# Two feed-forwards: GpSimd's products on the residual are put behind a copy that reads the last low part of x

## The chip, the cores and the metric

The kernel runs on one core of one Trainium2 chip. A core has a matrix engine (TensorE, PE in the profile, with its weight loads as PEld), a vector engine (VectorE, DVE), a scalar engine (ScalarE, ACT), GpSimd (POOL) and a queue engine that starts most transfers (SyncE, SP). The metric is the device time of one execution in microseconds (us).

## What is computed

Two layers of a decoder trunk on 512 tokens of width 1024, in float32. Each layer is a token mixer, a residual with a norm, a feed-forward, and again a residual with a norm:

```python
for i in range(DEPTH):                       # DEPTH = 2
    y = gla_mixer(h, ...) if i == 0 else gdn_mixer(h, ...)
    h = layer_norm(ALPHA * h + y, ln_g[i, 0], ln_b[i, 0])
    h = layer_norm(ALPHA * h + conv_ffn(h, ...), ln_g[i, 1], ln_b[i, 1])

def layer_norm(x, g, b):
    return (x - mean) * rsqrt(var + eps) * g + b

def conv_ffn(x, w_in, conv_w, w_out):        # 2 x 2816 columns
    gate, up = split(causal_dwconv(x @ w_in, conv_w))
    return (gelu(gate) * up) @ w_out
```

## The kernel before

**Number format.** TensorE is fed with two parts of each float32 number, a high part in a fast format (`xh`, `wh`) and a low part, the rest (`xl`, `wl`). A product is three matmuls: `xh` with `wh`, `xl` with `wh`, `xh` with `wl`. ScalarE makes the high part of a weight tile by a copy, and VectorE the low part by a subtraction (`split_out`, L732).

**Layout.** Tokens stand in four blocks of 128 (`tb`), the width in two halves of 512 columns (`hf`). The residual `h[tb][hf]` has tokens on the partitions. What the matmuls of the next stage read, `xh` and `xl`, has the width on the partitions, in eight chunks (`NC`), with all 512 tokens along the row.

**The norm (`ln`, L896 ff.).** It runs once for each block, when the mixer's output projection has added its sum into `h[tb]`. `ln_stats` makes mean and inverse root: statistics on VectorE (L884, L888), a square root on ScalarE (L886), and four small instructions on VectorE, one number for each partition (L892, L893, L894, L906). Then VectorE normalises half 0 (L908) and ScalarE half 1 (L907), TensorE transposes both (`xT`, L235), ScalarE multiplies by `g` and adds `b` on the way out of the accumulator (L925), one of the two engines writes `xh` (L929, L932), and VectorE writes `xl` (L933).

**The residual that is kept.** The `h` that the next residual needs is also to be multiplied by `g` and to get `b` added, with the columns along the row this time. After the mixers that is GpSimd's work: L949 multiplies `h[hf]` by a tile of `g` spread over all partitions, L950 adds the one of `b`, eight products and eight sums for each feed-forward. The four tiles of `g` and `b` (`gb`) are loaded by SyncE (L871) into slots of the feed-forward's stage. Nobody reads these `h` before the feed-forward's first group of output tiles is added into them, a hundred microseconds later. In the norm behind the first feed-forward (`spill`) the residual goes to memory instead, and GpSimd has no such work; behind the second the output is written.

**The start of a feed-forward.** TensorE's order is the program's. When the feed-forward begins (`fm_items`), the norms of blocks 2 and 3 are still to come: the first four column blocks of the weights (of 128 columns each, 24 matmuls) are first multiplied with tokens 0 to 255 only, matmuls of 128x256, and the transposes of blocks 2 and 3 stand in between, after the first 18 matmuls and after 18 more. Then the same four are multiplied with tokens 256 to 511, and from the fifth on a column block takes all 512 tokens at once. Behind each come ScalarE's first tap of the convolution out of the accumulator (L1037), two taps on VectorE (L1039), the gelu for a gate (L1057), and the product of gate and up (L1068). The weights go through four buffers of `wh` and `wl` (`WB`).

**Slots.** A feed-forward's stage has six slots of 128x512 (`FFN_SLOTS`), which the four `gb` tiles and the gates' `conv` tiles share. A tile that takes over a slot waits until its last reader has done.

**What sets the order.** The program issues the work from generators with a clock of its own, in which flags such as `("x", tb)` stand for finished steps. In `ln`, the GpSimd part of block `tb` is issued when all four flags of x are set and RESID_DELAY + 10 x `tb` of that clock have passed. The order in which an engine gets its instructions is then laid down by a planner that takes them when their data are ready by its own estimate; only TensorE's order is nailed to the program's. An engine runs its list in order, and each instruction waits, on the chip, for the data and tiles that it needs, whatever the program's clock had said. So a product of GpSimd can start as soon as its block is normalised and transposed and `g` has landed. `behind(a, b)` adds to the planner's rules that `a` comes after `b` on their engine; it adds no wait of its own.

Of the kernel before, what the change touches and what calls it, by code (L numbers as in the profile page):

```python
# [8 lines left out]
F32 = mybir.dt.float32  # L9
# [6 lines left out]
P = 128  # L16
D = 1024
S = 512
NTB = S // P
NC = D // P  # L20
# [50 lines left out]
def c4(t):  # L71
    return t.rearrange("p (c i) -> p c i", c=4)


def blk(i, n=P):
    return slice(i * n, i * n + n)


class Trunk:
# [818 lines left out]
    def ln(self, tb, spill=False):  # L898

        nc = self.nc  # L900
        li, h = self.li, self.h[tb]
        for hf in range(2):
            self.flags.pop(("h", tb, hf))
        mv, rs = self.ln_stats(tb)
        nb = self.small([P, 1], "ln_nb")
        nc.vector.scalar_tensor_tensor(nb, mv[:, 0:1], -1.0, rs, ALU.mult, ALU.mult)  # L906
        nc.scalar.activation(h[1], h[1], AF.Identity, bias=nb, scale=rs)  # L907
        normed = nc.vector.tensor_scalar(h[0], h[0], mv[:, 0:1], rs, op0=ALU.subtract, op1=ALU.mult)  # L908
        if self.due and tb < 2:
            if tb:  # L910
                self.behind(self.lows[3], normed)
            self.normed = normed
        ready = self.vec(0.65)
        yield ready - self.clk + 0.2
        for hf in range(2):
            ps = self.psum("xT")
            self.tr4(ps, h[hf])
            xf = self.slot("xf")
            for j in range(4):
                c = li * NC + 4 * hf + j  # L920
                if spill and hf and tb == NTB - 1:
                    nc.vector.tensor_scalar(xf[:, blk(j)], ps[:, blk(j)], self.lg[:, c:c + 1], self.lb[:, c:c + 1],
                                            op0=ALU.mult, op1=ALU.add)
                else:
                    nc.scalar.activation(xf[:, blk(j)], ps[:, blk(j)], AF.Identity,  # L925
                                         bias=self.lb[:, c:c + 1], scale=self.lg[:, c:c + 1])
            xs = (slice(None), slice(4 * hf, 4 * hf + 4), blk(tb))
            if hf == 0:
                nc.vector.tensor_copy(self.xh[xs], c4(xf))  # L929
                self.vec(0.42, self.clk + 1.8)  # L930
            else:
                nc.scalar.copy(self.xh[xs], c4(xf))  # L932
            nc.vector.tensor_sub(self.xl[xs], c4(xf), self.xh[xs])  # L933
            ready = self.vec(0.7, self.clk + (2.6 if hf else 0.0))
        self.set(("x", tb), max(0.1, ready - self.clk))
        yield 0.0

        self.spilled = spill
        if spill:
            for hf in range(2):  # L940
                nc.gpsimd.dma_start(self.hd[blk(tb), blk(hf, S)], h[hf])
            self.h[tb] = None
            return
        for i in range(NTB):
            yield from self.until(("x", i))
        yield RESID_DELAY + 10.0 * tb
        gb = self.ln_gb()
        for hf in range(2):
            nc.gpsimd.tensor_mul(h[hf], h[hf], gb[hf])  # L949
            nc.gpsimd.tensor_add(h[hf], h[hf], gb[2 + hf])  # L950
            self.set(("h", tb, hf))
            yield 5.0
# [1191 lines left out]
```

## Time and profile before

| | |
|---|---|
| median of the runs | 1217.89 us (1217.6 to 1219.16) |
| the profiled execution | 1219.53 us |
| its span, first to last instruction | 1217.8 us |
| granted clock of TensorE | 1.000 |
| first feed-forward's first matmul, second one's | 208.84 us, 855.56 us |
| GpSimd's products and sums (L949, L950), first feed-forward | 199.55 to 239.6 us |
| the same, second feed-forward | 854.31 to 888.9 us |

The page gives the busy time of each engine. The list of waits says who stood idle, and what ended it. A row of the timeline has the start in us, the length in us, the engine, the line of the kernel, the operation, the tile written and the tiles read, the shapes, and in brackets the idle time ahead of it with what ended that. Rows of the same kind that follow each other are drawn into one, with their count.

### The profile page before, as it was taken

To read this page: it belongs to the slowest core of one execution; us is meant where nothing else is said; L and a number is where in the kernel's file an instruction comes from. 1 tells how busy PE (TensorE), PEld (TensorE's weight loads), DVE (VectorE), ACT (ScalarE), POOL (GpSimd) and SP (SyncE) were. 2 spreads that over 40 slices of the span, in tenths; PEclk is the share of its full clock that TensorE was granted. 3 is DMA by queue.
4 is the path that set the end of the run, shared out by engine and by line. 5 is a ranking of instruction groups with operands and counts; after the bars stand their busy time and mean duration, and the time that the engine had idled before them with its cause. 6 is when DMAs were issued, how large, how long until landed. Compare 5 with 4: busy or idle time off the path is not lost.

```text
span 1217.8 us, 17218 instructions
## 1 busy us (share of the span) xinstructions
PE 1208.7 (99%) x6477; PEld 1020.4 (84%) x6477; DVE 928.2 (76%) x1527; ACT 628.3 (52%) x1116; POOL 170.9 (14%) x211
## 2 busy tenths in 40 slices
PE   9999999999999999999999999999999999999998
PEld 8888888988888888889888888988888888888886
DVE  6989787787757675766789969799697757775667
ACT  5666663544434443454678557864544433443440
POOL 3030101601100110001242032200610100020000
PEclk9999999999999999999999999999999999999999
DMA  8384652536743554433444356535444853383311
GB/s 234 111 168 112 136 155 71 186 109 138 190 121 94 123 95 121 127 99 90 122 127 130 90 136 105 118 125 143 154 119 106 180 164 102 103 176 88 112 60 69
DMA packets 177907, 152.55 MB, mean 125 GB/s; under 512 B 16966, under 2 KB 140938, under 8 KB 177824
## 3 DMA queue, kind: packets, MB, share of 16 engines
q1 hardware_dynamic: 161920, 115.23, 32.0%
q0 software_dynamic: 14944, 35.57, 15.3%
q8 instruction: 51, 0.84, 0.3%
q10 hardware_dynamic: 960, 0.66, 0.2%
q14 instruction: 32, 0.26, 0.1%
HBM read 133.06 MB, written 5.78 MB: 114 GB/s over the span
## 4 chain that ended last, share of the span: by engine, by line
PE 92%; DVE 5%; ACT 1%; DMA 1%; issue 1%; SPq 0%; DVEq 0%; POOL 0%; ACTq 0%; POOLq 0%
PE fm L217 51%; PE fold L217 22%; PE tm L217 11%; PE o L217 2%; DVE wl L732 1%; PE xT L235 1%; DVE conv L1640 1%; DVE tmp L1800 1%; PE pg L217 1%; PE vn L217 1%; PE yT L235 1%; DVE tt L1802 1%; PE V L217 0%; PE ds L217 0%; PE qs L217 0%
## 5 line engine op out<-in xcount | busy, mean ns | idle before, releaser
L217 PE MATMUL fm<-xh,wh 128*128 128x512 f32 (+2 forms) x1096 | 400.7, 368 | 0.7 <-ACT xh L732 0.7
L217 PE MATMUL fm<-xl,wh 128*128 128x512 f32 (+2 forms) x1096 | 399.0, 366 | 0.2 <-DVE xl L933 0.2
L217 PE MATMUL fm<-xh,wl 128*128 128x512 f32 (+1 forms) x1072 | 391.8, 367 | 0.0
L732 DVE TENSOR_TENSOR wl<-raw,wh 128x1024 fp32r<-128x1024 f32 (+1 forms) x156 | 195.0, 1252 | 139.3 <-ACT wh L732 139.2
L732 ACT CAST wh<-raw 128x1024 fp32r<-128x1024 f32 (+1 forms) x157 | 162.6, 1037 | 203.3 <-PE fm L217 124.4
L217 PEld LDWEIGHTS fm<-xh,wh 128*128 128x128 f32 (+1 forms) x1096 | 205.5, 188 | 34.0 <-ACT xh L732 0.9
L217 PEld LDWEIGHTS fm<-xl,wh 128*128 128x128 f32 (+1 forms) x1096 | 205.5, 188 | 33.2 <-DVE xl L933 0.5
L217 PEld LDWEIGHTS fm<-xh,wl 128*128 128x128 f32 x1072 | 201.3, 189 | 33.2
L1039 DVE SCALAR_TENSOR_TENSOR conv<-fm,ffn_cw,conv 128x511 f32<-128x511 f32 x112 | 83.5, 746 | 10.0 <-ACT conv L1037 8.4
L732 ACT CAST wh<-b 128x1024 fp32r<-128x1024 f32 x48 | 50.2, 1053 | 74.0 <-PE fold L217 34.0
L217 PE MATMUL fold<-wh,fh 128*128 128x512 f32 x224 | 87.7, 391 | 0.0
L217 PE MATMUL fold<-wl,fh 128*128 128x512 f32 x224 | 87.2, 390 | 0.0
L217 PE MATMUL fold<-wh,fl 128*128 128x512 f32 x224 | 87.2, 389 | 0.0
L732 DVE TENSOR_TENSOR wl<-b,wh 128x1024 fp32r<-128x1024 f32 x48 | 58.4, 1223 | 22.4 <-ACT wh L732 22.0
L417 POOL DMA_DIRECT2D b<-b x24 | 20.8, 915 | 354.6 <-DVE wl L732 309.9
L1057 ACT ACTIVATE conv<-conv 128x512 f32<-128x512 f32 x44 | 27.8, 631 | 66.0 <-DVE conv L1039 66.0
L1640 DVE SCALAR_TENSOR_TENSOR conv<-fm,gdn_cw,conv 128x511 f32<-128x511 f32 (+2 forms) x72 | 54.1, 789 | 8.1 <-ACT conv L1638 7.5
L217 PEld LDWEIGHTS fold<-wh,fh 128*128 128x128 f32 x224 | 42.1, 188 | 9.5 <-DVE h L1128 1.0
L217 PEld LDWEIGHTS fold<-wh,fl 128*128 128x128 f32 x224 | 42.1, 188 | 8.8
L217 PEld LDWEIGHTS fold<-wl,fh 128*128 128x128 f32 x224 | 42.1, 188 | 8.6
L1039 DVE SCALAR_TENSOR_TENSOR form<-fm,ffn_cw,form 128x511 f32<-128x511 f32 x64 | 47.7, 746 | 1.1
L217 PE MATMUL fold<-wh,xh 128*128 128x512 f32 x104 | 43.4, 417 | 0.2
(362 smaller groups left out, 2039.8 us busy)
## 6 DMA issues: line engine op xcount, KB each, us to landing
raw<-in_ffn_w_in_dram SPq DMA_DIRECT2D x88, 512.0 KB, 3.8
raw<-in_gdn_w_in_dram SPq DMA_DIRECT2D x28, 512.0 KB, 4.1
b<-in_ffn_w_out_dram SPq DMA_DIRECT2D x24, 512.0 KB, 5.8
b<-b POOLq DMA_DIRECT2D x24, 512.0 KB, 4.7
raw<-in_ffn_w_out_dram SPq DMA_DIRECT2D x20, 512.0 KB, 3.7
raw<-in_gla_w_in_dram SPq DMA_DIRECT2D x18, 512.0 KB, 4.1
gw<-in_gla_w_in_dram POOLq DMA_DIRECT2D x8, 512.0 KB, 7.2
raw<-in_gla_w_out_dram SPq DMA_DIRECT2D x8, 512.0 KB, 4.2
```

What stands on the lines that cost most here:

```text
L217: t = self.nc.tensor.matmul(out, a, b, start=start, stop=stop, skip_group_check=joined)
L235: t = self.nc.tensor.transpose(out, a, self.ident[:n, :n])
L417: self.nc.gpsimd.dma_start(out, group[src, i][:, cols], accum_op=ALU.add)
L732: return self.nc.scalar.copy(dst_h, src), self.nc.vector.tensor_sub(dst_l, src, dst_h)
L1039: nc.vector.scalar_tensor_tensor(a[:, d:], ps[:, :S - d], tap(2 - d), a[:, d:], ALU.mult, ALU.add)
L1057: nc.scalar.activation(a, a, AF.Gelu)
L1640: self.conv = nc.vector.scalar_tensor_tensor(a[:, d:], ps[:, :S - d], tap(3 - d), a[:, d:], ALU.mult, ALU.add)
L1800: nc.vector.tensor_tensor(tv, m3[:, j, j + 1:].unsqueeze(2).to_broadcast([P, n, m]), t3[:, j, :m].unsqueeze(1).to_broadcast([P, n, m]), AL ...
L1802: nc.vector.tensor_add(t3[:, j + 1:, :m], t3[:, j + 1:, :m], tv)
```

## The change

For block 0 the generator first issues a copy of one column, on GpSimd, into a small tile of its own. It reads the last token of the last chunk of `xl`, which the norm of block 3 writes (L933). Each of the eight products (L949) is placed behind this copy on GpSimd; the sums follow their products as before. It holds for the norms behind both mixers, so for both feed-forwards.

```diff
         gb = self.ln_gb()
+        if tb == 0:
+            self.gate = nc.gpsimd.tensor_copy(self.small([P, 1], "gate"), self.xl[:, NC - 1, S - 1:].bitcast(F32))
         for hf in range(2):
-            nc.gpsimd.tensor_mul(h[hf], h[hf], gb[hf])
+            self.behind(nc.gpsimd.tensor_mul(h[hf], h[hf], gb[hf]), self.gate)
             nc.gpsimd.tensor_add(h[hf], h[hf], gb[2 + hf])
```

## The prediction, on record before the result

> **What bounds the kernel now.** I read the page first, then who waited for whom on TensorE, then the timelines of the four engines around each start of a feed-forward. The page says where a gain can be at all:
>
> ```profile
> PE 1208.7 (99%) x6477; PEld 1020.4 (84%) x6477; DVE 928.2 (76%) x1527; ACT 628.3 (52%) x1116; POOL 170.9 (14%) x211
> ```
>
> TensorE is busy for 1208.7 of 1217.8 us. GpSimd, whose products are moved, is busy for 14% and never bounds by itself. So the change can only pay where GpSimd makes somebody late for whom TensorE then waits. The list of TensorE's waits, longest first, begins with
>
> ```profile
> PE xT L235 <- DVE h L908: 1.8, 1, 1.8
> ```
>
> one wait of 1.8 us of the transposes `xT` for the normalised residual `h`, written by VectorE at L908. The timeline puts it at 858 us, where the second feed-forward begins while the norm of its input is still running for the last two blocks of 128 tokens. VectorE there (start, us, engine, line):
>
> ```profile
> 846.57 0.22 DVE L893 SCALAR_TENSOR_TENSOR ln_t<-ln_rs,ln_var 128x1 f32<-128x1 f32 x1
> 846.82 0.16 DVE L894 SCALAR_TENSOR_TENSOR ln_rs<-ln_t,ln_rs 128x1 f32<-128x1 f32 x1
> 847.01 0.16 DVE L906 SCALAR_TENSOR_TENSOR ln_nb<-ln_mv,ln_rs 128x1 f32<-128x1 f32 x1
> 847.09 0.54 DVE L908 TENSOR_SCALAR h<-h,ln_mv,ln_rs 128x512 f32<-128x512 f32 x1
> ...
> 854.13 0.16 DVE L892 RECIPROCAL ln_rs<-ln_root 128x1 f32<-128x1 f32 x1 [0.42 <-ACT ln_root L886]
> 854.33 1.28 DVE L893 SCALAR_TENSOR_TENSOR ln_t<-ln_rs,ln_var 128x1 f32<-128x1 f32 x1
> 855.64 1.23 DVE L894 SCALAR_TENSOR_TENSOR ln_rs<-ln_t,ln_rs 128x1 f32<-128x1 f32 x1
> 856.79 0.68 DVE L933 TENSOR_TENSOR xl<-xf,xh 128x512 fp32r<-128x512 f32 x1
> 857.39 1.23 DVE L906 SCALAR_TENSOR_TENSOR ln_nb<-ln_mv,ln_rs 128x1 f32<-128x1 f32 x1
> 858.54 1.57 DVE L908 TENSOR_SCALAR h<-h,ln_mv,ln_rs 128x512 f32<-128x512 f32 x1
> ```
>
> The same four lines are there twice. For block 1 (from 846.57) they take 0.22, 0.16, 0.16 and 0.54 us; for block 2 (from 854.33) they take 1.28, 1.23, 1.23 and 1.57 us, with one element per partition in three of them. Data cannot explain that. GpSimd does: in just these microseconds it runs four of the products that the change moves.
>
> ```profile
> 854.31 5.52 POOL L949 TENSOR_TENSOR h<-h,gb 128x512 f32<-128x512 f32 x4 [63.71 <-DVE ln_rs L892]
> ```
>
> 5.52 us for four is 1.38 us each, so the products end at about 855.7, 857.1, 858.5 and 859.8, and VectorE's stretched instructions end at 855.6, 856.9, 858.6 and 860.1: VectorE gets on when a product ends. The Trainium skill (SBUF — State Buffer, section "Who interferes with whom") says that VectorE and GpSimd share one pair of SBUF ports and that whichever starts first holds it for its whole instruction; the ends above agree.
>
> **What is removed, in the second feed-forward.** TensorE there and, as the yardstick, at the start of the first feed-forward, where the same order of matmuls and transposes met no wait:
>
> ```profile
> 855.56 0.28 PE L217 MATMUL fm<-xh,wh 128*128 128x256 f32 x1
> ...
> 858.10 0.28 PE L217 MATMUL fm<-xh,wl 128*128 128x256 f32 x1
> 860.17 1.09 PE L235 MATMUL xT<-ident,h 128*128 128x128 f32 x8 [1.79 <-DVE h L908]
> ...
> 864.21 0.36 PE L217 MATMUL fm<-xh,wh 128*128 128x256 f32 x1
> ```
>
> ```profile
> 208.84 0.28 PE L217 MATMUL fm<-xh,wh 128*128 128x256 f32 x1
> ...
> 210.99 1.04 PE L235 MATMUL xT<-ident,h 128*128 128x128 f32 x8
> ...
> 214.80 0.36 PE L217 MATMUL fm<-xh,wh 128*128 128x256 f32 x1
> ```
>
> Between the first `fm` matmul and the third run of them (36 matmuls of 128x256 and 16 transposes) the second feed-forward takes 864.21 - 855.56 = 8.65 us, the first 214.80 - 208.84 = 5.96 us. The difference, **2.69 us**, is what the stall costs; it is more than the 1.8 us of the wait list, because starts count also a short wait for `xl` (written at 856.79) and a short one before the second transposes, and the list counts idle time against modelled ends. I take the 2.69.
>
> Does it all come back? Without products beside it block 2's chain starts at 854.13, when ScalarE's root is there (ScalarE is not touched), and takes 0.16 + 0.22 + 0.16 + 0.68 + 0.16 + 0.54 = 1.9 us: VectorE's half of `h` is done at about 856.1. The transposes want it at 855.56 + (210.99 - 208.84) = 857.71 and came at 860.17. So 1.6 us of cover stand where 2.46 us were missing; ScalarE's half, which starts when L906 ends, has a little less. What is late next is nothing on this path: block 3's norm follows 2.4 us earlier than before too.
>
> In the first feed-forward the products already end up between VectorE's instructions without making TensorE wait (5.96 us, the bare time): nothing to win there, 0.
>
> **What is added.** One copy of a 128x1 on GpSimd per feed-forward. The nearest row is the same instruction at the start of the kernel:
>
> ```profile
> L1366 POOL COPY gk<-xl 128x1 f32<-128x1 f32 x1 | 0.6, 582 | 4.0 <-DVE xl L732 4.0
> ```
>
> 0.58 us on an idle engine; at worst it holds VectorE for as long once, after the last `xl`, when VectorE has nothing to do until the next weight's cast. On the path 0.
>
> **What is moved.** All eight products and eight sums of a feed-forward now queue behind the copy on GpSimd. Nothing else is queued there: the next instructions of GpSimd are the additions of the folded weights, a whole group of tiles later. SyncE's loads of `gb`, and those of the weights behind them, wait for tiles that the norms free, not for GpSimd. The cost is that GpSimd finishes later, and two things look at that: VectorE, beside which it now runs longer, and the slots of `g` and `b`, which come free later. The rows of the second feed-forward's sixteen:
>
> ```profile
> L950 POOL TENSOR_TENSOR h<-h,gb 128x512 f32<-128x512 f32 x8 | 12.8, 1617 | 10.0 <-DMA gb<-in_ln_b_dram 10.0
> L949 POOL TENSOR_TENSOR h<-h,gb 128x512 f32<-128x512 f32 x8 | 12.0, 1531 | 63.7 <-DVE ln_rs L892 63.7
> ```
>
> 24.8 us in all, in either feed-forward. I work it through in the first, where TensorE's times will not move:
>
> ```profile
> 220.50 1.08 DVE L933 TENSOR_TENSOR xl<-xf,xh 128x512 fp32r<-128x512 f32 x1 [0.90 <-ACT xh L932]
> ...
> 236.83 3.90 DVE L732 TENSOR_TENSOR wl<-raw,wh 128x1024 fp32r<-128x1024 f32 x2
> ...
> 244.19 1.22 DVE L732 TENSOR_TENSOR wl<-raw,wh 128x1024 fp32r<-128x1024 f32 x1
> ```
>
> ```profile
> 235.93 3.71 POOL L950 TENSOR_TENSOR h<-h,gb 128x512 f32<-128x512 f32 x2
> ```
>
> ```profile
> 233.59 0.40 PE L217 MATMUL fm<-xh,wh 128*128 128x512 f32 x1
> ...
> 239.06 0.39 PE L217 MATMUL fm<-xh,wh 128*128 128x512 f32 x1
> ```
>
> The last `xl` would end at 220.50 + 0.68 = 221.2, the copy at 221.8, the sixteen at 246.6 instead of 239.6. In these 7 us VectorE is contended where it was not. A weight split (L732) takes 1.95 us beside GpSimd (3.90 for two) and 1.22 without, so 0.7 each; if all its instructions there went the same way it would lose 7 x (1 - 1.22/1.95) = 2.6 us. That is the value I take; the ends are 0 and 7 us. By the Trainium skill's rule the loser stands still for the whole of the other's instruction, which would put it nearer to the 7 than to the 2.6; by the one as by the other the next paragraph decides.
>
> The cover is the lead of the weights. TensorE takes up its fifth weight at 233.59 and the next one 5.47 us later (239.06), so the ninth at 255.5; its low half, first needed two matmuls later, is the split of 244.19, done at 245.4. The lead is 10 us. Minus 2.6 it is 7.5, minus 7 it is 3. The seventh and eighth weights (236.83) ran beside GpSimd before as they will after, with the seventh, done at 238.8, needed at 244.5 + 0.4: 6 us ahead. So this costs 0, and if the cover were gone up to 7 us in each feed-forward.
>
> The slots: the stage has six (FFN_SLOTS), four hold `g` and `b`, two are left for the `conv` tiles of the gates. ScalarE writes these in L1037:
>
> ```profile
> 231.73 0.67 ACT L1037 ACTIVATE conv<-fm,ffn_cw 128x512 f32<-128x512 f32 x1
> ...
> 239.98 0.68 ACT L1037 ACTIVATE conv<-fm,ffn_cw 128x512 f32<-128x512 f32 x1
> ```
>
> The third one (239.98) stands in a slot of `g` in the program of before, free once the 13th of the sixteen has read it: after the change at 221.8 + 13 x 24.8/16 = 242.0. ScalarE is held for 2 us, and VectorE reads this tile only after the split of 244.19. Hidden: 0.
>
> **Sum.** 2.69 - 0 - 0 = 2.69 us. The profiled execution took 1219.53 us around its span of 1217.8; it becomes 1216.8 around 1215.1. The median of the runs shown is 1217.89, which is close to the bare span, so I take the same off it: **1215.2 us**. Its own spread is 0.4 us from the yardstick and as much again from the runs (1217.6 to 1219.16): 1214.4 to 1216.0.
>
> **Rivals.** First, the gain is hidden anyway: the stretch after 864 us may be paced by something with a clock of its own, the stream of weights say, and gives the 2.69 us back. 1217.9. For it: VectorE and the queues are the less idle the earlier TensorE asks. Against: after 864 us TensorE's list has only a short wait at the very end, and its weights are loaded when TensorE has freed a tile, so they move with it. 0.09.
>
> Second, the change doesn't do what it says: the copy is released by an earlier writer of that corner of `xl`, or the planner leaves products ahead of it. Then the four products meet the norm as before and the copy is 0.58 us on an idle engine: 1217.9. Against: the copy is issued after all four blocks' flags. 0.06.
>
> Third, slower than before: the planner, seeing the products end later, gives the second gate's `conv` (231.73) a slot of `g`. ScalarE would stand from 231.73 to 242.0, with the casts of the seventh and eighth weight queued behind it, 10.3 us where the seventh has 6 us: TensorE loses 4.3 us in each feed-forward, less the 2.7 won: +5.9, **1223.8**. It decides from a hold of 6 us, a slot free after 237.7. Against: before, that tile was written while GpSimd still worked on every one of its tiles, so it had a slot of its own, and the count of slots is the same. 0.05.
>
> **How the numbers follow.** The forecast has 0.80, the rivals 0.09, 0.06 and 0.05. 0.2% of the median, about what a measurement of this kernel can tell from no change, is 2.44 us, only a quarter of a microsecond under my sum: of the forecast's 0.80 I put 0.57 beyond it and 0.23 within. With the first two rivals "same" is 0.38, and "slower" 0.05. The forecast's own range holds some 0.7; to leave out no more than 2 in 10 the range goes up to the two cases of no change, 1214.4 to 1217.9.
>
> **What would show it.** Right: TensorE's list has no wait for L908; L893, L894 and L906 are back at 0.16 to 0.22 us in the second feed-forward's norms; first `fm` to third run takes 6.0 us there; GpSimd's first product comes after a copy of 0.6 us and after the last `xl`; the sixteen end some 25 us later without a gap; weight splits stay stretched for longer, and TensorE does not wait for one. Wrong: a new wait of TensorE for a `wl` or `wh`, or a long idle time of ScalarE before a `conv` of L1037; or the stall gone and the time the same.

## The result and the profile after

The changed kernel takes **1221.05 us** (median of 12 runs, 1220.52 to 1221.48) against 1218.53 us (1217.6 to 1220.83) for the kernel before in the same comparison: a ratio of 1.0019 [1.001, 1.0028], 2.5 us slower. The profiled execution took 1221.48 us around a span of 1219.7 us, at a granted clock of 1.000 as before.

The stall that the change was aimed at is gone. TensorE's list of waits, whole, has no line of L908:

```profile
PE warm L814 <- POOL one L104: 1.0, 1, 1.0
PE fm L217 <- ACT xh L732: 0.7, 1, 0.7
PE mid L217 <- ACT diag L967: 0.6, 1, 0.6
PE V L217 <- DMA T<-dinvt: 0.2, 1, 0.2
```

VectorE in the norm of block 2, in front of the second feed-forward; these rows answer to those from 854.13 us before:

```profile
857.29 0.16 DVE L892 RECIPROCAL ln_rs<-ln_root 128x1 f32<-128x1 f32 x1 [0.43 <-ACT ln_root L886]
857.49 0.22 DVE L893 SCALAR_TENSOR_TENSOR ln_t<-ln_rs,ln_var 128x1 f32<-128x1 f32 x1
857.74 0.16 DVE L894 SCALAR_TENSOR_TENSOR ln_rs<-ln_t,ln_rs 128x1 f32<-128x1 f32 x1
857.82 0.68 DVE L933 TENSOR_TENSOR xl<-xf,xh 128x512 fp32r<-128x512 f32 x1
858.42 0.15 DVE L906 SCALAR_TENSOR_TENSOR ln_nb<-ln_mv,ln_rs 128x1 f32<-128x1 f32 x1
858.49 0.54 DVE L908 TENSOR_SCALAR h<-h,ln_mv,ln_rs 128x512 f32<-128x512 f32 x1
```

L893, L894, L906 and L908 take 0.22, 0.16, 0.15 and 0.54 us in place of 1.28, 1.23, 1.23 and 1.57. GpSimd starts later, behind the copy (L949; the products are now L951, the sums L952):

```profile
869.82 0.18 POOL L949 COPY gate<-xl 128x1 f32<-128x1 f32 x1 [75.85 <-DVE xl L933]
869.97 5.06 POOL L951 TENSOR_TENSOR h<-h,gb 128x512 f32<-128x512 f32 x4
...
892.11 3.18 POOL L952 TENSOR_TENSOR h<-h,gb 128x512 f32<-128x512 f32 x2
```

And TensorE goes from the first `fm` matmul to the third run of them without a gap, in 864.31 - 858.34 = 5.97 us, where it took 8.65:

```profile
858.34 0.28 PE L217 MATMUL fm<-xh,wh 128*128 128x256 f32 x1
...
860.50 1.04 PE L235 MATMUL xT<-ident,h 128*128 128x128 f32 x8
...
864.31 0.36 PE L217 MATMUL fm<-xh,wh 128*128 128x256 f32 x1
```

So 2.68 us came back at this place, and yet the kernel is slower. Where the time went is read by setting the chain of waits of the two kernels side by side: the order of TensorE's instructions is the program's in both, so the difference of the starts of the same piece is the delay gathered by then. Rows are start, length (us), engine and tile, line, count. Before:

```profile
75.67 20.45 PE fold L217 x90
167.69 31.33 PE tm L217 x138
215.04 84.02 PE fm L217 x444
299.06 32.64 PE fold L217 x144
424.29 32.64 PE fold L217 x144
864.45 84.02 PE fm L217 x444
948.47 32.64 PE fold L217 x144
1073.72 32.64 PE fold L217 x144
```

After:

```profile
76.47 20.89 PE fold L217 x90
169.23 31.78 PE tm L217 x138
217.03 84.02 PE fm L217 x444
301.05 33.47 PE fold L217 x144
427.15 33.47 PE fold L217 x144
864.55 84.02 PE fm L217 x444
948.57 33.47 PE fold L217 x144
1074.71 33.47 PE fold L217 x144
```

Two things are to be seen. The delay is +0.80 us at the first row, +1.99 when the first feed-forward's `fm` begins, still +1.99 after its 444 matmuls, +2.86 at the second `fold` stage, +0.10 behind the stall that went, and +0.99 at the last row. (The second `fold` stage adds to the +2.86, and ahead of the stall about 1 us comes back in the second layer's mixer, GDN: half of it in its output projection, of which more below, and half around its products `V`, whose wait for a transfer is 0.6 us in the list before and 0.2 us after.) And apart from 0.67 us that stand already at 10 us, the delay grows only inside certain groups: 144 `fold` matmuls of a feed-forward's output projection take 33.47 us in place of 32.64, 232.4 ns each in place of 226.7, with no wait anywhere, while the 444 `fm` matmuls take 84.02 us in both. The four such stages cost about 0.85 us each, nearly all of it in the 144 matmuls. The groups by line (matmuls, then busy us, mean ns of one, idle time ahead) say the same: `fold<-wh,fh` goes from 87.7 to 88.4 us of busy time for 224 matmuls (first row before, second after), and the two other groups on `fh` and `fl` from 87.2 to 88.4:

```profile
L217 PE MATMUL fold<-wh,fh 128*128 128x512 f32 x224 | 87.7, 391 | 0.0
L217 PE MATMUL fold<-wh,fh 128*128 128x512 f32 x224 | 88.4, 395 | 0.0
```

Nothing about these matmuls was edited. What differs is where their data lie. The copy writes a tile of a name of its own, `gate`: four buffers of 32 bytes per partition in the pool of small tiles. That pool is laid out ahead of the stages' pool, so every tile of every stage starts 128 bytes further on (its base goes from 117888 to 118016), while the weight buffers, `xh`, `xl` and the residual stay. `fh`, `fl` (feed-forwards), `xfh` and `yh` (mixers) lie in a stage; `xh` and `xl` do not, and `fm` is not slowed. In `fold` and in the mixers' output projections the stage's tile is the operand that is loaded into TensorE and the weight buffer is the one that streams through it, the moving operand; in `fm` the weight buffer is loaded and `xh` or `xl` streams.

### The profile page after: what moved, and what is told of

It reads as the page before. It is cut to its first block, busy times and chain, and to the rows that moved or that the text cites. A ratio compares the mean times of both kernels' runs of the same rounds, so it can differ in the third digit from the quotient of the medians.

```text
span 1219.7 us, 17214 instructions
## 1 busy us (share of the span) xinstructions
PE 1213.0 (99%) x6477; PEld 1021.2 (84%) x6477; DVE 924.5 (76%) x1527; ACT 629.0 (52%) x1116; POOL 172.7 (14%) x213
## 4 chain that ended last, share of the span: by engine, by line
PE 98%; DVE 1%; DMA 0%; issue 0%; SPq 0%; ACT 0%; DVEq 0%; POOL 0%; ACTq 0%; POOLq 0%
PE fm L217 54%; PE fold L217 22%; PE tm L217 13%; PE o L217 2%; PE xT L235 1%; PE pg L217 1%; PE vn L217 1%; PE yT L235 1%; PE V L217 0%; PE ds L217 0%; PE pq L217 0%; PE qs L217 0%; PE ks L217 0%; PE s L217 0%; PE warm L814 0%; PE sa L217 0%
## 5 line engine op out<-in xcount | busy, mean ns | idle before, releaser
L217 PE MATMUL fold<-wh,fh 128*128 128x512 f32 x224 | 88.4, 395 | 0.0
L217 PE MATMUL fold<-wh,fl 128*128 128x512 f32 x224 | 88.4, 395 | 0.0
L217 PE MATMUL fold<-wl,fh 128*128 128x512 f32 x224 | 88.4, 395 | 0.0
L732 ACT CAST fh<-form 128x1792 fp32r<-128x1792 f32 (+3 forms) x24 | 28.7, 1194 | 30.1 <-DVE form L1082 19.0
```

What stands on the lines that cost most here:

```text
L217: t = self.nc.tensor.matmul(out, a, b, start=start, stop=stop, skip_group_check=joined)
L732: return self.nc.scalar.copy(dst_h, src), self.nc.vector.tensor_sub(dst_l, src, dst_h)
```

## The experiments

**Place (P)**: a 128x512 matmul is some 6 ns slower when its two operands, the loaded and the moving one, do not start at the same address modulo 256 bytes, and the new tile made that so. **GpSimd (G)**: the products, which run later and longer beside the rest, slow TensorE or its feeders. P speaks of the tile and G of the order of the work, so each can be had without the other.

The table has what the traces gave. The distance is (stage tiles - weight buffers) modulo 256, in the feed-forwards and GLA / in GDN, from the addresses at which the tiles were put. The two columns of ns are the mean from start to start of consecutive matmuls: the `fold` stages of the feed-forwards, and the output projections of GLA / GDN. The stall is the first `fm` to the third run in the second feed-forward.

| kernel | distance | fold | GLA / GDN | stall, us |
|---|---|---|---|---|
| before | 0 / 128 | 226.8 | 227.2 / 233.2 | 8.65 |
| after | 128 / 0 | 232.5 | 232.5 / 227.4 | 5.97 |
| e1_realigned | 0 / 128 | 226.8 | 227.2 / 233.1 | 5.97 |
| e2_shift128 | 128 / 0 | 232.5 | 232.3 / 227.1 | 7.88 |
| e3_shift256 | 0 / 128 | 226.8 | 227.2 / 233.2 | 7.94 |
| e4_shift64 | 64 / 192 | 233.3 | 233.3 / 229.2 | 6.87 |
| e5_second_only | 0 / 128 | 226.9 | 227.0 / 233.1 | 5.97 |
| e6_gdn_aligned | 0 / 0 | 226.8 | 227.1 / 227.4 | 5.96 |
| e7_no_new_tile | 0 / 128 | 226.9 | 227.0 / 233.0 | 5.97 |
| e8_wts128 | 128 / 0 | 232.5 | 232.4 / 227.1 | 7.84 |

**The order of the change, the stages back on the same distance: e1_realigned.** Eight buffers of `gate` move the stages by 256 bytes and not by 128.

```diff
-self.gate = nc.gpsimd.tensor_copy(self.small([P, 1], "gate"), ...)
+self.gate = nc.gpsimd.tensor_copy(self.small([P, 1], "gate", bufs=8), ...)
```

> The changed kernel with eight buffers for the copy's tile in place of four: the same instructions in the same order, but every tile of a stage lies 256 bytes later in its partition than before the change, not 128. Theory P (place): the change lost its gain because its new tile moved the stages' tiles by 128 bytes against the weight buffers, and a matmul whose two operands differ by 128 modulo 256 bytes goes at 232.4 ns instead of 226.8. Then the fold's matmuls go back to 226.8 ns, the stall of the second feed-forward stays away, and the time is 2.7 us under the kernel before (1215.8 for 1218.5). Theory G (GpSimd): the products that run later, or the copy, slow TensorE. Then nothing changes against the changed kernel: 2.5 us over the kernel before, the fold at 232.

1216.96 us against 1218.89, 0.9984 [0.9976, 0.9993]: faster than before by 1.9 us, where 2.7 were expected. The chain has the old pace with the new order:

```profile
299.68 32.64 PE fold L217 x144
424.93 32.64 PE fold L217 x144
...
861.94 84.01 PE fm L217 x444
945.95 32.64 PE fold L217 x144
1071.20 32.64 PE fold L217 x144
```

G falls: GpSimd works as late and as long here as in the changed kernel (its sixteen run behind the copy without a gap, from 220.74 to 246.02 us in the first feed-forward). Four more buffers of a tile that nobody else reads take 4.4 us off the span (1219.7 to 1215.3).

**The place alone, without the change: e2_shift128, e3_shift256, e4_shift64.** In the kernel before, more buffers of a small tile that is there already; no instruction is added or moved.

```diff
-nb = self.small([P, 1], "ln_nb")
+nb = self.small([P, 1], "ln_nb", bufs=8)    # e2; 12 in e3, 6 in e4
```

> The kernel before, with eight buffers instead of four for the norm's small tile ln_nb: no copy, no gate, the same instructions, and the stages' tiles 128 bytes later, as in the changed kernel. Theory P: the fold's 672 matmuls of both feed-forwards and the 192 of the first mixer's folded gate lose 5.6 ns each (4.8 us), the output projections of the two mixers lose and win half a microsecond, and the stall of 2.7 us stays: 4.8 us over the kernel before, 1223.3 for 1218.5. Theory G: no difference, 1218.5.

1223.55 us against 1218.89, 1.004 [1.0026, 1.0054]: 4.7 us slower by 128 bytes alone. Its chain has the pace of the changed kernel, and its list of TensorE's waits the old stall:

```profile
300.30 33.47 PE fold L217 x144
426.44 33.47 PE fold L217 x144
```

```profile
PE xT L235 <- DVE h L908: 1.5, 1, 1.5
```

> The kernel before with twelve buffers for ln_nb: 256 bytes later, no other edit. Theory P, in the form that only the distance modulo 256 bytes counts: the kernel before to the tenth of a per cent (1218.5), the fold at 226.8 ns. If instead any move, or the fuller memory, costs something: 2 to 5 us over it. Theory G: 1218.5 too; this one is the control to the run with 128 bytes.

1218.79 us against 1218.89, 0.9998 [0.9989, 1.0007]: 256 bytes cost nothing that can be measured.

```profile
299.42 32.64 PE fold L217 x144
424.68 32.64 PE fold L217 x144
```

So it is neither a longer pool nor a shift as such. A half of the 128 was tried to see whether the cost grows with the distance:

> The kernel before with six buffers for ln_nb: the stages' tiles 64 bytes later (192 modulo 256, the weight buffers 128). Is it the distance, or in which half of 256 bytes a tile begins? If the half: fold at 226.8 ns, 1218.5. If any distance that isn't a multiple of 256: 232.4 ns and 4.8 us over the kernel before. If it goes with the distance: between, 229 to 230 ns and about 2.4 us over.

1223.64 us against 1218.75, 1.0044 [1.003, 1.0058]; the 144 take 33.60 us, 233.3 ns each:

```profile
300.98 33.60 PE fold L217 x144
427.26 33.60 PE fold L217 x144
```

64 bytes cost as much as 128, the second of the three readings. It doesn't hold for every distance alike: GDN, at a distance of 192 here, went at 229.2 ns, between the two paces.

**The distance or the address: e8_wts128.** In the kernel before, a small constant goes into another pool, and so the weight buffers, the residual and the buffers of the raw weights move by 128 bytes; the stages, `xh` and `xl` stay.

```diff
-ones = self.keep([P, 32], "one")
+ones = ap.tile([P, 32], F32, name="one", tag="one")
```

> The kernel before with the 128-byte tile of ones moved ahead of the weight buffers, so that wh, wl, the residual and the loads lie 128 bytes later, x and all stages' tiles where they were; no other edit. Theory P: now the feed-forwards' and projections' fm matmuls (xh against wh) are the ones that differ by 128 bytes: 2518 of 128x512 at 5.6 ns are 14.1 us, some 750 of 128x256 between 0 and as much each (0 to 4.2 us), and the folds with 128x512 some 6.4 us: 20 to 25 us over the kernel before, 1239 to 1243, and the fm pace at 232.4 ns. Theory G, or that only the place of the stages' tiles matters: 1218.5.

1236.71 us against 1218.89, 1.0147 [1.0134, 1.016]. With the stages where they were, `fold` goes at the slow pace; and now the `fm` groups pay too, which read `xh` and `xl` against weights that have moved (before: 84.02 us for the 444, and 400.7, 399.0 and 391.8 us of busy time). Of what was moved, these matmuls read the weight buffers alone:

```profile
217.63 85.44 PE fm L217 x444
L217 PE MATMUL fm<-xh,wh 128*128 128x512 f32 (+2 forms) x1096 | 404.9, 372 | 0.7 <-ACT xh L732 0.7
L217 PE MATMUL fm<-xl,wh 128*128 128x512 f32 (+2 forms) x1096 | 403.0, 370 | 0.0
L217 PE MATMUL fm<-xh,wl 128*128 128x512 f32 (+1 forms) x1072 | 396.0, 371 | 0.0
```

It is the distance between the two operands and not the address of one. The size, 17.8 us, came out below the 20 to 25 that were expected. The matmuls of 128x256 at the start of each feed-forward paid nothing: their groups' means lie between 119 and 123 ns in every kernel, this one too. But the 20 had nothing for them already. Of the rest the traces show 0.8 us in the stall, which was shorter here (7.84 for 8.65), and 0.5 in GDN, which came onto the weights' distance; what else is missing is not known.

**No new tile: e7_no_new_tile.** The changed kernel, with the copy writing into a tile name that is there already.

```diff
-self.small([P, 1], "gate")
+self.small([P, 1], "ln_nb")
```

> The changed kernel with one edit: the copy writes into a buffer of the norm's small tile ln_nb, so that no tile is new and every stage's tile lies where it lay before the change. Theory P (place): the fold at 226.8 ns, the stall away, 1.5 to 2.7 us under the kernel before, as with the move by 256 bytes. Theory G (the late products or the copy slow TensorE): 2.5 us over it. A third reading, that the run with 256 bytes won by something else in its place in memory, would leave this one at the kernel before or over it.

1216.85 us against 1218.75, 0.9985 [0.9976, 0.9993]: the same time as e1_realigned's without a byte moved.

```profile
299.18 32.64 PE fold L217 x144
...
945.54 32.64 PE fold L217 x144
```

**Only the second feed-forward: e5_second_only.** e1_realigned, with copy and rule only for the norms of the second layer.

```diff
-if tb == 0:
+if tb == 0 and li == 2:
...
-self.behind(nc.gpsimd.tensor_mul(h[hf], h[hf], gb[hf]), self.gate)
+product = nc.gpsimd.tensor_mul(h[hf], h[hf], gb[hf])
+if li == 2:
+    self.behind(product, self.gate)
```

> The changed kernel with eight buffers for the copy's tile (stages 256 bytes later) and the gate in the second feed-forward alone; in the first the products start when they can, as before. The prediction's step that the first feed-forward has nothing to win: as the run with both gates and 256 bytes, 1.5 to 2.7 us under the kernel before, and TensorE's time from the first fm matmul to the third run 6.0 us in both. If the gate in the first gave part of that gain, this one is slower than that by that part; if it cost something there, faster.

1216.64 us against 1218.75, 0.9987 [0.9978, 0.9995]; e7_no_new_tile, beside it, 1216.85. The first feed-forward's part of the change does nothing that can be measured; TensorE's time to the third run is 5.96 us in the first feed-forward and 5.97 in the second.

**All stages on the weights' distance: e6_gdn_aligned.** GDN's tiles lay at 128 in the kernel before, behind an odd number of small tiles of its own; e1_realigned with one of these made 128 bytes longer.

```diff
-bn, bp, rk, nb = keep("gd_bn"), keep("gd_bp"), keep("gd_rk"), keep("gd_nb")
+bn, bp, rk, nb = keep("gd_bn"), keep("gd_bp"), keep("gd_rk"), self.own([P, 2 * DH, 4], "gd_nb")[:, :DH]
```

> The changed kernel with eight buffers for the copy's tile, and one small tile of the second mixer's stage widened by 128 bytes, so that this stage's slots too lie at 128 modulo 256 like the weight buffers (they lie at 0 in the kernel before). Theory P: on top of the 256-byte run, the 96 matmuls of that mixer's output projection that read wh and wl against yh and yl go from 232.5 to 227 ns: 0.5 us in the trace, too little for the timed runs to tell; in all 2 to 3.2 us under the kernel before. Theory G: 2.5 us over it.

1216.37 us against 1218.75, 0.9979 [0.997, 0.9988]: the lowest of all, though its interval overlaps those of e5_second_only and e7_no_new_tile. The stretch itself shows the gain. The output projection of GDN in the chain of e7_no_new_tile, and then of e6_gdn_aligned:

```profile
814.38 31.12 PE tm L217 x135
```

```profile
814.40 30.63 PE tm L217 x135
```

0.49 us off these 135 matmuls, by the place of their stage's slots alone.

## Why the prediction was wrong

**The step that failed** is "What is added", with its "On the path 0". It priced the copy as an instruction, by its duration, and not the tile that it writes by its place. The place cost (1219.7 - 1215.3) = 4.4 us of span between the changed kernel and e1_realigned, where I had 0. By stage, from before and after: the four `fold` stages 0.85 us each, 3.4 us in all; the first mixer, GLA, 1.99 - 0.67 = 1.3 us (0.67 is the delay that stood already at 10 us: the same early run of 40 `fm` matmuls starts at 9.85 us before and at 10.52 after, and between 9.80 and 10.52 us in the ten traces, in e1_realigned at 10.46); GDN came back with about 0.5 us, since the same 128 bytes put its tiles on the weights' distance. 3.4 + 1.3 - 0.5 = 4.2 us of the 4.4.

**The removal was right in kind and place, and its term too large for the median.** TensorE's stretch went to 5.97 us, the bare time that I had set. But the 2.69 us came from one execution, which with 1219.53 us stood 1.6 us over the median that I took them off, and the kernel before doesn't lose the same in each. With the old order the stretch took 8.65, 7.94, 7.88, 7.84 and 6.87 us in five traces, 0.9 to 2.7 us over the bare 5.96. It goes by how many instructions of the norm's chain meet a product: VectorE has four stretched ones in the kernel before, where GpSimd's first product starts 0.02 us ahead of L893; three in e2_shift128, e3_shift256 and e8_wts128, where it starts 0.12 to 0.26 us behind L893; and two in e4_shift64, 0.63 us behind. In the medians the order alone is worth 1.9 us (e1_realigned, e7_no_new_tile) or 2.1 (e5_second_only). With the order's 1.9 and the place's 4.4 the sum is +2.5, as measured. Of the 5.85 us between the forecast of 1215.2 and 1221.05, then, 4.4 are the place, 0.8 the size of the removal, and 0.6 the kernel before, whose median was 1218.53 beside the changed one and not 1217.89.

**The rest of the working held.** The first feed-forward has nothing to win (e5_second_only). The sixteen run without a gap behind the copy, in 25.5 us, and the ninth weight's low half comes after them:

```profile
221.97 0.18 POOL L949 COPY gate<-xl 128x1 f32<-128x1 f32 x1 [90.15 <-DVE xl L933]
222.11 5.06 POOL L951 TENSOR_TENSOR h<-h,gb 128x512 f32<-128x512 f32 x4
...
244.28 3.17 POOL L952 TENSOR_TENSOR h<-h,gb 128x512 f32<-128x512 f32 x2
```

```profile
248.11 1.22 DVE L732 TENSOR_TENSOR wl<-raw,wh 128x1024 fp32r<-128x1024 f32 x1
```

Before, that split began at 244.19. 1.99 of the 3.92 us are TensorE's own delay by then, which leaves 1.93 us for the longer contention, nearer to the 2.6 that I took than to the 7 that I had as the far end. The product of gate and up just ahead of it (L1068, after the change L1070), for one, takes 1.48 us beside GpSimd and took 0.69 without. The split is done at 249.3 and wanted at 255.5 + 2.0 = 257.5: 8 us of lead left for the 7.5 predicted, and no wait of TensorE for a weight. ScalarE's hold for the slot of `g` is there, 1.03 us for the 2 predicted, and as well hidden:

```profile
243.09 0.69 ACT L1039 ACTIVATE conv<-fm,ffn_cw 128x512 f32<-128x512 f32 x1 [1.03 <-POOL h L951]
```

The copy took 0.18 us, not 0.58.

**The rivals** were three, and none was it. The third had the right sign by a mechanism that didn't happen: the second gate kept a slot of its own. The first had the right shape, a gain that is given back, but after 864 us there is no clock that gives it back; the loss lies in stages 90 us and more away, the greater part of it ahead of the stall. The last line of the prediction, "the stall gone and the time the same", comes nearest to what the trace showed (the time was 2.5 us longer), and I had no mechanism for it.

**What stays open.** That the distance sets the pace is shown by kernels that move one or the other operand; by what mechanism is not. TensorE's weight loads run beside its matmuls (PEld was busy for 1021.2 us and PE for 1213.0 us of the changed kernel's 1219.7), so the runs don't separate a matmul's own loaded operand from the one that is loaded beside it for the next. Distances other than 0, 64, 128 and 192 were not tried, 192 in one stage only, and why 64 costs as much as 128 is not known.

## What to carry to other kernels

A new small tile is never only its instruction: it moves every tile that is laid out behind it, and where TensorE is busy for 99% of the span, 6 ns for each of several hundred matmuls outweigh a stall of 2 us. Let an added helper write into a tile that is there already, or fill its buffers up to 256 bytes, and compare the pace of the matmuls in stages that the edit doesn't touch before a change of order is judged by its time. And a stall that hangs on which engine came first by some tenths of a us should be sized from several executions.

## What the runs showed of the hardware

The pace of a 128x512 matmul followed the distance of its two operands in SBUF: 226.8 ns from start to start where the loaded and the moving operand begin at the same address modulo 256 bytes, 232.5 ns at a distance of 128, 233.3 at 64, and 229.2 in the one stage at 192; it came at a granted clock of 0.999 to 1.000 and with no wait of these matmuls in the list. The 128x256 matmuls showed nothing of it, 119 to 123 ns at a distance of 0 and of 128. The Trainium skill (SBUF — State Buffer, section "Who interferes with whom") gives TensorE two read ports, one for the moving operand and one for the weight load, independent of each other, and says that TensorE never waits on anyone. It speaks of the engines and not of addresses. Read as a rule on TensorE's own two operands too, it would let the 144 matmuls of a stage take 32.64 us wherever the tiles lie; measured were 33.47 us, so read like that it doesn't hold here, and no other engine is shown to be the cause.

The same section of the Trainium skill says that a VectorE instruction with two inputs in SBUF contends with a GpSimd one that reads SBUF. That agrees: L893 on two numbers of each partition took 1.28 us beside the products and 0.22 us without them.
